# Forming mean, epsilon and scale of the norms on ScalarE instead of GpSimd, in a one-core hybrid conformer and attention block

## The chip, the cores and the metric

The kernel runs on one core of one Trainium2 chip. A core has a matrix engine (TensorE; PE in the profile, with its weight loads as PEld), VectorE (DVE), ScalarE (ACT), GpSimd (POOL) and a queue that issues DMAs (SyncE, SP). Each engine works through its own instructions in order; semaphores make one wait for another. The metric is the device time of one execution in microseconds, as the median of several.

## The reference, cut to what matters

One layer over 512 tokens of width 1024, everything in float32:

```python
h = rms_norm(x, g_pre_mix) * (1 + scale1) + shift1
z = h @ w_in                      # GLU | q latent | kv latent | rotary key | two gates
u = causal_depthwise_conv(glu)    # 31 taps
u = silu(layer_norm(u))           # over the 1024 channels
y_a = u @ w_conv_out
q = rms_norm(q_lat) @ w_uq ; kv = rms_norm(kv_lat) @ w_ukv
y_b = attention(q, kv) @ w_attn_out
y = (g_a * y_a + g_b * y_b) @ w_out
x = x + gate1 * rms_norm(y, g_post_mix)
h = rms_norm(x, g_pre_mlp) * (1 + scale2) + shift2
x = x + gate2 * rms_norm(relu(h @ w_mlp_in)**2 @ w_mlp_out, g_post_mlp)
# rms_norm: y * rsqrt(mean(y*y) + 1e-6) * g ;  layer_norm: (u - mean) * rsqrt(var + 1e-6) * g + b
```

So there are four kinds of RMS norm (of x, of the two latents, of the mixer's output and of the new x, of the MLP's output) and one layer norm.

## The kernel before, in words

Tokens are worked on in NT = 4 tiles of 128. Every large product is done as three float32r matmuls (high by high, high by low, low by high), for which ACT rounds each operand to its high part (a CAST) and DVE subtracts to get the low part. The work runs: norm of x; its transposes; first products with w_in; the latents and the rest of the GLU; attention over 8 heads; w_attn_out; the two gate products (GB, then GA); the layer norm of the convolution; w_conv_out; w_out; the post-mixer norm and the pre-MLP norm; the MLP in four chunks; the last norm and the output.

The 31-tap convolution runs on DVE as 248 multiply-adds of 128x512, each reading two operands from SBUF, spread through everything from the latents to the layer norm.

The order of instructions is not written by hand. `emit` records every operation with its regions read and written; `Planner.plan` simulates the five engines with the costs of `Planner.cost` and picks, for each engine, the ready operation with the earliest due time (for PE, the lowest rank; `plan.boost` moves operations ahead). It repeats this up to nine times with the buffer lifetimes of the pass before, keeps the shortest plan, and `issue` writes the instructions in that order. All of them come from line 388, so the profile tells them apart by tile and shape alone. In the planner's costs a small GpSimd operation is 160 ns (460 ns for a power), a small ACT operation 93 ns, and 150 ns pass until another engine may go on.

What the change touches:

- `rstd` (line 507): turns a sum of squares into 1/sqrt(sum*scale + base). GpSimd does a `tensor_scalar` (multiply, add) and then a `tensor_tensor` with the power -0.5. The sums come from ACT (`Square` with `accum_out`; in the trace an ACTIVATE followed by an ACTIVATION_READ_ACCUMULATOR). The consumers are DVE, except for the latents, where ACT multiplies.
- The two-part norms at lines 1381 and 1576: one GpSimd `tensor_scalar` forms the first half's sum times the scale plus epsilon (`s[:, 2:3]`), and `rstd` takes that as its base.
- `ln_stats` (line 1214): the statistics of the layer norm's first six channel blocks. For the first four, ACT copies the transposed block with `accum_out=sA`; GpSimd multiplies the sum by -1/512 into `ns`; ACT then squares with `ns` as its bias. PE's transposes for it are boosted (line 1270), so that they stand early in PE's order, between the matmuls of the gate products.
- `layer_norm` (line 1228) closes the statistics on DVE, takes one power of 128x4 on GpSimd, and forms the scale and shift that DVE and ACT apply.

Tiles by name: `stats` holds the sums of the RMS norms, `lns` those of the layer norm, `nhalf` the constant -0.5, `f_arena` and `r_arena` the float32 and float32r buffers.

Of the kernel before, what the change touches and what calls it, by code (L numbers as in the profile page):

```python
# [11 lines left out]
F32 = mybir.dt.float32  # L12
R32 = mybir.dt.float32r
I32 = mybir.dt.int32
AF = mybir.ActivationFunctionType
ALU = mybir.AluOpType

P = 128
T = 512
NT = T // P  # L20
D = 1024
# [371 lines left out]
def tile_hybrid_block(  # L393
# [35 lines left out]
    nc.gpsimd.memset(ones, 1.0)  # L429
    nhalf = const.tile([P, 8], F32, name="nhalf")  # L430
    nc.gpsimd.memset(nhalf, -0.5)
    mask = const.tile([P, T], F32, name="mask")
    nc.gpsimd.memset(mask, 0.0)
    nc.gpsimd.affine_select(out=mask[:, T - P:], in_=mask[:, T - P:], compare_op=ALU.is_ge, fill=1e30,
# [5 lines left out]
    def emit(past, replay):  # L440
# [63 lines left out]
            assert st_n[0] <= 96  # L504
            return st[:, a:a + n]

        def rstd(o, ssq, scale, base=EPS):

            n = o.shape[1]
            pool.tensor_scalar(o, ssq, scale, base, ALU.mult, ALU.add)  # L510
            pool.tensor_tensor(o, o, nhalf[:, :n], ALU.pow)


# [688 lines left out]
        pump(KD * TAPS)  # L1202
        vT = []

        lns = tile_of([P, 12, NT], F32, "lns")
        sA, ns, qA, dB, qB, dC, qC, dm, va, rs, nb, tq = (lns[:, i] for i in range(12))

        def ln_in(t, c0, n):
            b = pb.alloc()
# [4 lines left out]
        def ln_stats(c0, n, d, q):  # L1214

            for t in range(NT):
                b = ln_in(t, c0, n)
                j = ra.alloc(n * P)
                if d is None:
                    act.activation(ra.v(j), pb.v(b, n * P), AF.Copy, accum_out=sA[:, t:t + 1])  # L1220
                    pool.tensor_scalar(ns[:, t:t + 1], sA[:, t:t + 1], -1.0 / (n * P), None, ALU.mult)
                else:
                    act.activation(ra.v(j), pb.v(b, n * P), AF.Identity, bias=ns[:, t:t + 1], accum_out=d[:, t:t + 1])
                act.activation(ra.v(j), pb.v(b, n * P), AF.Square, bias=ns[:, t:t + 1], accum_out=q[:, t:t + 1])
                ra.free(j)
                pb.free(b)
# [142 lines left out]
        for tp in range(2):  # L1369
            xn = []  # L1370
            for t in (2 * tp, 2 * tp + 1):
                for k in range(KD):
                    mm3(pb.v(ys[t, 1]), yl(t, k), wo[k // 2](k % 2, 0, 512), k == 0, k == KD - 1)
                    if t == NT - 1 and k % 2 == 1:
                        wo[k // 2].free()
                s = stat(6)
                j = fa.alloc(512)
                for nh in range(2):
                    act.activation(fa.v(j), pb.v(ys[t, nh]), AF.Square, accum_out=s[:, nh:nh + 1])
                fa.free(j)  # L1380
                pool.tensor_scalar(s[:, 2:3], s[:, 0:1], 0.25 / D, EPS, ALU.mult, ALU.add)
                rstd(s[:, 3:4], s[:, 1:2], 0.25 / D, s[:, 2:3])
                y = fa.alloc(D)
                for nh in range(2):
                    sl = slice(nh * 512, (nh + 1) * 512)
                    dve.scalar_tensor_tensor(fa.v(y)[:, sl], pb.v(ys[t, nh]), s[:, 3:4], fa.v(G1)[:, sl], op0=ALU.mult, op1=ALU.mult)
                    pb.free(ys[t, nh])
                dve.tensor_tensor(fa.v(xr[t]), fa.v(xr[t]), fa.v(y), ALU.add)
                act.activation(fa.v(y), fa.v(xr[t]), AF.Square, accum_out=s[:, 4:5])
                rstd(s[:, 5:6], s[:, 4:5], 1.0 / D)  # L1390
                dve.tensor_scalar(fa.v(y), fa.v(xr[t]), s[:, 5:6], None, ALU.mult)
                sp.dma_start(out=xD[t], in_=fa.v(xr[t]))
                fa.free(xr[t])
                xn.append(y)
            if tp == 1:
                for m in mT:
                    ra.free(*m)
                ws0[0, 1] = wunit(w_mlp_in, 4, 0, 4, 256)
                ws0.update(hid_weights(0, 4, 2))
            if tp == 0:  # L1400
                h2[:] = [pair(T) for _ in range(KD)]
            hsl = slice(tp * 256, (tp + 1) * 256)
            for k2 in range(KD // 2):
                b = pb.alloc()
                for q in range(2):
                    for t in range(2):
                        k = 2 * k2 + q
                        pe.transpose(pb.v(b)[:, (2 * q + t) * P:(2 * q + t + 1) * P], fa.v(xn[t])[:, k * P:(k + 1) * P], ident)
                for q in range(2):
                    k = 2 * k2 + q  # L1410
                    ps, v = pb.v(b)[:, q * 256:(q + 1) * 256], fa.alloc(256)
                    hb, lb = h2[k]
                    if k == 0:
                        act.activation(ra.v(hb)[:, hsl], ps, AF.Identity, scale=mod[:, 3, k:k + 1], bias=mod[:, 2, k:k + 1])
                        dve.tensor_scalar(fa.v(v), ps, mod[:, 3, k:k + 1], mod[:, 2, k:k + 1], ALU.mult, ALU.add)
                    else:
                        act.activation(fa.v(v), ps, AF.Identity, scale=mod[:, 3, k:k + 1], bias=mod[:, 2, k:k + 1])
                        act.copy(ra.v(hb)[:, hsl], fa.v(v))
                    dve.tensor_tensor(ra.v(lb)[:, hsl], fa.v(v), rf(hb)[:, hsl], ALU.subtract)
                    fa.free(v)  # L1420
                pb.free(b)
            fa.free(*xn)
# [99 lines left out]
        for ch in range(NCH):  # L1522
# [32 lines left out]
            def banked(mi, nh, bs):  # L1555
# [3 lines left out]
                for tt in range(2):  # L1559
                    t = 2 * mi + tt  # L1560
                    y = fa.v(ysb[t])[:, sl]
                    if ch == 0 and n == 1:
                        act.copy(y, pb.v(bs[tt]))
                    else:
                        dve.tensor_tensor(y, pb.v(bs[tt]), y, ALU.add)
                    if ch < NCH - 1 or not done:
                        continue
                    s = fin[t]
                    i = seen[t] = seen.get(t, -1) + 1
                    j = ra.alloc(512)  # L1570
                    act.activation(ra.v(j), y, AF.Square, accum_out=s[:, i:i + 1])
                    ra.free(j)
                    dve.tensor_tensor(y, y, fa.v(G2)[:, sl], ALU.mult)
                    if i == 0:
                        continue
                    pool.tensor_scalar(s[:, 2:3], s[:, 0:1], 1.0 / D, EPS, ALU.mult, ALU.add)
                    rstd(s[:, 3:4], s[:, 1:2], 1.0 / D, s[:, 2:3])
                    xb = load(D, xD[t])
                    for hf in range(2):
                        sh = slice(hf * 512, (hf + 1) * 512)  # L1580
                        dve.scalar_tensor_tensor(fa.v(ysb[t])[:, sh], fa.v(ysb[t])[:, sh], s[:, 3:4], fa.v(xb)[:, sh],
                                                 op0=ALU.mult, op1=ALU.add)
                        sp.dma_start(out=out[t * P:(t + 1) * P, sh], in_=fa.v(ysb[t])[:, sh])
# [50 lines left out]
```

## Time and profile before

| | |
|---|---|
| median of 3 runs | 838.59 us (838.47 to 839.24) |
| the profiled execution | 836.4 us, its span 834.6 us |
| busy in the span | PE 808.1 us (97%), DVE 685.2 (82%), ACT 415.5 (50%), POOL 45.4 (5%) |
| DMA | 117.28 MB, mean 141 GB/s |
| chain that ended last | PE 85%, DMA 4%, DVE 3%, POOL 2%, ACT 2% |

The span is the time from the first to the last instruction on the core. Busy time is read by stage, because the share over the span averages stages with different limits; what counts for an edit is which engine PE was waiting for in the stage where the edit lies.

### The profile page before, as it was taken

The page shows a single profiled execution, that of the slowest core. Times are in us where ns is not written, and L with a number is a line of the kernel's source. Part 1 is how long each engine was busy: PE and PEld are TensorE (multiplying, and loading weights), DVE is VectorE, ACT ScalarE, POOL GpSimd, SP SyncE. Part 2 cuts the span into 40 slices and gives each one's busy share as a digit, 9 for nine tenths or more (in the row PEclk, how much of TensorE's full clock was granted, in tenths as well). Part 3 has the DMA queues.
Part 4 walks back from the last instruction along what each step waited for, and adds up shares of the span by engine and source line. Part 5 has one row for each costly group of instructions (what it writes and reads, how often), then busy time and mean ns, then how long its engine had stood idle before and what let it go on. Part 6 is the DMA issues. An engine that isn't in the chain of part 4 may idle for free.

```text
span 834.6 us, 10659 instructions
## 1 busy us (share of the span) xinstructions
PE 808.1 (97%) x3940; PEld 675.7 (81%) x3940; DVE 685.2 (82%) x1012; ACT 415.5 (50%) x680; POOL 45.4 (5%) x119
## 2 busy tenths in 40 slices
PE   6999999999999989999999989999999999999995
PEld 3777888899988868888888779888888888888884
DVE  4979979999999997999999779298529993975696
ACT  5463363375893346227434287375346544553641
POOL 3001040000000020000000230000000000000002
PEclk9999999999999999999999989999999999999998
DMA  9997423202353141332799650064014831660302
GB/s 310 336 311 234 148 69 98 67 27 77 101 177 102 51 128 49 101 111 91 233 353 363 210 201 27 26 202 152 0 51 132 290 132 51 197 206 1 101 1 101
DMA packets 86823, 117.28 MB, mean 141 GB/s; under 512 B 7274, under 2 KB 60627, under 8 KB 86770
## 3 DMA queue, kind: packets, MB, share of 16 engines
q1 hardware_dynamic: 86770, 116.59, 43.5%
q8 instruction: 31, 0.51, 0.2%
q14 instruction: 22, 0.18, 0.1%
HBM read 108.18 MB, written 8.39 MB: 140 GB/s over the span
## 4 chain that ended last, share of the span: by engine, by line
PE 85%; DMA 4%; DVE 3%; POOL 2%; issue 2%; ACT 2%; SPq 1%; DVEq 0%; POOLq 0%; ACTq 0%
PE psum L388 85%; DMA f_arena<-in_w_in_dram 4%; DVE f_arena L388 3%; SPq L388 1%; POOL stats L388 1%; ACT f_arena L388 1%; DMA f_arena<-in_x_dram 1%; ACT r_arena L388 1%; POOL lns L388 1%; DVE r_arena L388 0%; DVEq L1629 0%; POOLq L1629 0%; DMA rows<-in_kv_norm_g_dram 0%; DVE mod L388 0%; DVE cols L388 0%
## 5 line engine op out<-in xcount | busy, mean ns | idle before, releaser
L388 PE MATMUL psum<-r_arena 128*128 128x512 f32 (+2 forms) x3592 | 766.5, 374 | 4.0 <-ACT r_arena L388 2.5
L388 PEld LDWEIGHTS psum<-r_arena 128*128 128x128 f32 x3592 | 634.4, 190 | 121.0 <-ACT r_arena L388 3.6
L388 DVE TENSOR_TENSOR r_arena<-f_arena,r_arena 128x1024 fp32r<-128x1024 f32 (+4 forms) x232 | 247.9, 1090 | 97.1 <-PE psum L388 48.5
L388 ACT CAST r_arena<-f_arena 128x1024 fp32r<-128x1024 f32 (+4 forms) x222 | 209.7, 966 | 183.3 <-PE psum L388 111.5
L388 DVE SCALAR_TENSOR_TENSOR f_arena<-f_arena,cw 128x512 f32<-128x512 f32 x240 | 164.8, 743 | 0.0
L388 ACT ACTIVATE f_arena<-psum 128x512 f32<-128x512 f32 x64 | 38.0, 597 | 119.6 <-PE psum L388 111.3
L388 DVE TENSOR_TENSOR f_arena<-f_arena 128x1024 f32<-128x1024 f32 (+3 forms) x78 | 77.0, 1003 | 8.3 <-ACT f_arena L388 6.3
L388 ACT ACTIVATE f_arena<-f_arena 128x512 f32<-128x512 f32 (+3 forms) x100 | 58.5, 604 | 20.2 <-DVE f_arena L388 19.4
L388 DVE SCALAR_TENSOR_TENSOR f_arena<-f_arena,cT 128x256 f32<-128x256 f32 (+2 forms) x84 | 55.2, 699 | 0.1
L388 PE MATMUL psum<-ident,f_arena 128*128 128x128 f32 (+1 forms) x240 | 35.3, 288 | 11.7 <-DVE f_arena L388 7.7
L388 PEld LDWEIGHTS psum<-ident,f_arena 128*128 128x128 f32 (+1 forms) x240 | 29.2, 148 | 17.2 <-DVE f_arena L388 8.7
L388 POOL TENSOR_SCALAR stats<-stats 128x1 f32<-128x1 f32 x32 | 14.8, 463 | 467.0 <-ACT r_arena L388 361.6
L388 DVE TENSOR_TENSOR f_arena<-psum,f_arena 128x512 f32<-128x512 f32 x52 | 35.2, 684 | 4.2 <-PE psum L388 3.9
L388 ACT CAST r_arena<-psum 128x512 fp32r<-128x512 f32 (+2 forms) x57 | 30.2, 566 | 15.8 <-PE psum L388 15.4
L388 DVE TENSOR_TENSOR r_arena<-psum,r_arena 128x512 fp32r<-128x512 f32 (+2 forms) x57 | 35.7, 656 | 2.2 <-ACT r_arena L388 1.9
L388 ACT COPY f_arena<-psum 128x512 f32<-128x512 f32 (+4 forms) x42 | 19.9, 500 | 23.0 <-PE psum L388 22.7
L388 ACT ACTIVATE r_arena<-f_arena 128x512 fp32r<-128x512 f32 (+3 forms) x20 | 13.0, 648 | 21.9 <-DVE f_arena L388 18.8
L388 DVE CUSTOM_DVE_ANT_0 f_arena<-psum,mask 128x128 f32<-128x128 f32 (+3 forms) x32 | 15.0, 484 | 2.5 <-PE psum L388 2.5
L388 POOL TENSOR_SCALAR lns<-lns 128x1 f32<-128x1 f32 x4 | 5.3, 1326 | 198.5 <-ACT r_arena L388 198.5
L388 POOL TENSOR_TENSOR stats<-stats,nhalf 128x1 f32<-128x1 f32 x24 | 15.2, 633 | 1.9
L388 DVE TENSOR_SCALAR f_arena<-f_arena,stats 128x1024 f32<-128x1024 f32 x8 | 6.0, 754 | 9.9 <-POOL stats L388 9.7
L388 DVE SCALAR_TENSOR_TENSOR f_arena<-f_arena 128x512 f32<-128x512 f32 (+1 forms) x18 | 13.1, 742 | 0.0
(93 smaller groups left out, 195.4 us busy)
## 6 DMA issues: line engine op xcount, KB each, us to landing
f_arena<-in_w_ada_dram SPq DMA_DIRECT2D x16, 1024.0 KB, 5.6
f_arena<-in_w_mlp_in_dram SPq DMA_DIRECT2D x32, 512.0 KB, 5.1
f_arena<-in_w_mlp_out_dram SPq DMA_DIRECT2D x32, 512.0 KB, 5.2
f_arena<-in_w_in_dram SPq DMA_DIRECT2D x28, 512.0 KB, 4.9
f_arena<-in_x_dram SPq DMA_DIRECT2D x8, 512.0 KB, 5.3
f_arena<-in_w_ada_dram SPq DMA_DIRECT2D x16, 256.0 KB, 5.7
f_arena<-in_w_ada_dram SPq DMA_DIRECT2D x8, 512.0 KB, 6.7
h_spill<-r_arena SPq DMA_DIRECT2D x16, 256.0 KB, 5.4
```

Source lines behind the costliest of these rows:

```text
L388: getattr(self.real[o.eng], o.fn)(*o.a, **o.k)
```

## The change

GpSimd keeps the power alone; scaling and adding epsilon go to ACT as an `Identity` activation with a scale and a bias read from SBUF, directly behind the accumulation that made the sum. A constant tile `epsc` holds epsilon. In the layer norm's statistics the factor -1/512 goes into the copy itself, so that its accumulated sum is the negative mean and no operation follows.

```diff
+    epsc = const.tile([P, 1], F32, name="epsc")
+    nc.gpsimd.memset(epsc, EPS)
...
-        def rstd(o, ssq, scale, base=EPS):
+        def rstd(o, ssq, scale, base=None):
             n = o.shape[1]
-            pool.tensor_scalar(o, ssq, scale, base, ALU.mult, ALU.add)
+            act.activation(o, ssq, AF.Identity, scale=scale, bias=epsc[:, 0:1] if base is None else base)
             pool.tensor_tensor(o, o, nhalf[:, :n], ALU.pow)
...
                 if d is None:
-                    act.activation(ra.v(j), pb.v(b, n * P), AF.Copy, accum_out=sA[:, t:t + 1])
-                    pool.tensor_scalar(ns[:, t:t + 1], sA[:, t:t + 1], -1.0 / (n * P), None, ALU.mult)
+                    act.activation(ra.v(j), pb.v(b, n * P), AF.Copy, scale=-1.0 / (n * P), accum_out=ns[:, t:t + 1])
...
-                pool.tensor_scalar(s[:, 2:3], s[:, 0:1], 0.25 / D, EPS, ALU.mult, ALU.add)
+                act.activation(s[:, 2:3], s[:, 0:1], AF.Identity, scale=0.25 / D, bias=epsc[:, 0:1])
                 rstd(s[:, 3:4], s[:, 1:2], 0.25 / D, s[:, 2:3])
...
-                    pool.tensor_scalar(s[:, 2:3], s[:, 0:1], 1.0 / D, EPS, ALU.mult, ALU.add)
+                    act.activation(s[:, 2:3], s[:, 0:1], AF.Identity, scale=1.0 / D, bias=epsc[:, 0:1])
                     rstd(s[:, 3:4], s[:, 1:2], 1.0 / D, s[:, 2:3])
```

The tile `lns` loses its row `sA`. Nothing else in the source is changed, but the planner lays out every engine's order anew.

## Rows read from the trace of the kernel before

**Rows 1.** Busy time by stage: stretch, length, engines (instructions), PE clock, DMA share, GB/s.

```profile
0.00:68.00 68.00, 59.17 (x270) 43.61 (x270) 50.02 (x119) 36.81 (x52) 7.75 (x58) 1.00 1.00 313
68.00:247.00 179.00, 178.72 (x1044) 157.94 (x1044) 166.54 (x329) 99.03 (x217) 12.46 (x24) 1.00 0.35 107
306.00:313.00 7.00, 3.00 (x16) 2.17 (x16) 5.42 (x8) 2.13 (x6) 4.62 (x1) 1.00 0.06 7
463.00:493.00 30.00, 27.18 (x128) 21.68 (x128) 21.74 (x30) 14.61 (x34) 8.27 (x15) 0.97 0.56 187
493.00:816.00 323.00, 323.00 (x1509) 271.88 (x1509) 235.25 (x238) 166.40 (x211) 3.27 (x6) 0.99 0.34 107
```

**Rows 2.** Timeline at the first layer-norm statistics: start, length, instructions [idle before, releaser].

```profile
302.26 8.03 DVE L388 SCALAR_TENSOR_TENSOR f_arena<-f_arena,cw 128x512 f32<-128x512 f32 x12
306.62 0.20 ACT L388 ACTIVATION_READ_ACCUMULATOR r_arena<-psum 128x1 f32 x1
306.90 4.62 POOL L388 TENSOR_SCALAR lns<-lns 128x1 f32<-128x1 f32 x1 [191.51 <-ACT r_arena L388]
310.21 1.22 DVE L388 TENSOR_TENSOR r_arena<-f_arena,r_arena 128x1024 fp32r<-128x1024 f32 x1
311.56 0.69 ACT L388 ACTIVATE r_arena<-psum,lns 128x512 fp32r<-128x512 f32 x1 [4.74 <-POOL lns L388]
312.39 1.14 PE L388 MATMUL psum<-ident,f_arena 128*128 128x128 f32 x8 [4.00 <-ACT r_arena L388]
316.29 1.23 DVE L388 TENSOR_TENSOR r_arena<-f_arena,r_arena 128x1024 fp32r<-128x1024 f32 x1 [4.87 <-ACT r_arena L388]
```

**Rows 3.** The stretch right behind that wait, columns as in rows 1.

```profile
312.39:318.00 5.61, 5.61 (x24) 4.58 (x25) 1.71 (x3) 3.87 (x10) 0.41 (x2) 0.70 0.34 93
```

**Rows 4.** Timeline of GpSimd alone, later in the span.

```profile
379.40 2.03 POOL L388 TENSOR_TENSOR lns<-lns,nhalf 128x4 f32<-128x4 f32 x1 [60.24 <-DVE lns L388]
...
807.84 0.19 POOL L388 TENSOR_SCALAR stats<-stats 128x1 f32<-128x1 f32 x1 [309.61 <-ACT r_arena L388]
```

**Rows 5.** Groups of instructions by form, of GpSimd and of ACT: busy, mean ns.

```profile
L388 POOL TENSOR_SCALAR stats<-stats 128x1 f32<-128x1 f32 x32 | 14.8, 463 | 467.0 <-ACT r_arena L388 361.6 <-ACT f_arena L388 103.7 <-ACT tmp L388 0.6
...
L388 ACT ACTIVATE f_arena<-ident,lns 128x128 f32<-128x128 f32 x4 | 1.3, 390 | 0.6 <-DVE lns L388 0.6
...
L388 ACT ACTIVATE tmp<-cT 128x8 f32<-128x8 f32 x1 | 0.2, 193 | 0.0
```

**Rows 6.** Timeline at the end of the layer norm.

```profile
366.26 4.71 DVE L388 SCALAR_TENSOR_TENSOR f_arena<-f_arena,cw 128x512 f32<-128x512 f32 x7
...
372.17 0.60 PE L388 MATMUL psum<-ident,f_arena 128*128 128x128 f32 x4
...
379.23 1.29 DVE L388 SCALAR_TENSOR_TENSOR f_arena<-f_arena 128x512 f32<-128x512 f32 x2
...
381.46 0.28 DVE L388 TENSOR_SCALAR f_arena<-ident,lns 128x128 f32<-128x128 f32 x1 [0.94 <-POOL lns L388]
...
381.89 2.02 PE L388 MATMUL psum<-f_arena,ones 128*128 128x128 f32 x16
```

**Rows 7.** Two stretches around the pre-MLP norm, columns as in rows 1.

```profile
488.00:493.00 5.00, 2.58 (x11) 1.65 (x10) 3.93 (x6) 5.00 (x15) 2.59 (x4) 0.82 0.79 260
491.00:498.20 7.20, 6.65 (x30) 6.25 (x31) 5.76 (x11) 6.77 (x13) 2.85 (x4) 0.53 0.73 254
```

**Rows 8.** Timeline of the last norm, up to the last DVE work.

```profile
828.00 0.19 ACT L388 ACTIVATION_READ_ACCUMULATOR r_arena<-f_arena 128x1 f32 x1
828.22 0.69 DVE L388 TENSOR_TENSOR f_arena<-f_arena 128x512 f32<-128x512 f32 x1 [0.79 <-ACT r_arena L388]
828.29 0.76 POOL L388 TENSOR_SCALAR stats<-stats 128x1 f32<-128x1 f32 x1 [3.65 <-ACT r_arena L388]
829.13 0.54 POOL L388 TENSOR_TENSOR stats<-stats,nhalf 128x1 f32<-128x1 f32 x1
829.71 1.42 DVE L388 SCALAR_TENSOR_TENSOR f_arena<-f_arena,stats 128x512 f32<-128x512 f32 x2 [0.79 <-POOL stats L388]
```

More of the change, by code (lines that the diff above doesn't have):

```diff
@@ L1203, in emit @@
         vT = []
-        lns = tile_of([P, 12, NT], F32, "lns")
-        sA, ns, qA, dB, qB, dC, qC, dm, va, rs, nb, tq = (lns[:, i] for i in range(12))
+        lns = tile_of([P, 11, NT], F32, "lns")
+        ns, qA, dB, qB, dC, qC, dm, va, rs, nb, tq = (lns[:, i] for i in range(11))
         def ln_in(t, c0, n):
```

## Prediction, made before the result was known

> **What bounds the kernel.** I first read busy time stage by stage [rows 1]. From 68 us on, PE is the kernel: it works 178.72 of 179.00 us through the latents and attention, and all 323.00 us of the MLP. Nothing done for ACT or GpSimd in such a stage can move the end. Four places are left: the first 68 us, where the DMA share is 1.00 and PE works 59.17 us; the seven microseconds from 306 to 313, where PE works only 3.00; the post-mixer and pre-MLP norms from 463 to 493, where it works 27.18 of 30.00; and the tail after the last matmul.
>
> Next I read the timeline of the odd seven microseconds [rows 2]. ACT finishes the sum of the first 128x512 block at 306.82. GpSimd takes it at 306.90 and needs 4.62 us for one multiplication of 128x1. ACT waits 4.74 us for that, PE 4.00 us for ACT (its transposes need what ACT holds), and DVE afterwards 4.87 us for ACT. Why 4.62? The 32 operations of the same form on `stats` take 0.46 us in the mean [rows 5], and one takes 0.19. What runs beside it is DVE: twelve multiply-adds with two operands in SBUF without a gap from 302.26 to 310.29, then a subtraction with two such operands to 311.43. GpSimd ends at 311.52, 0.09 us behind the last of them. So I read the 4.62 us as GpSimd kept out while DVE runs two-operand instructions back to back.
>
> What marks this place is the consumer. `ns` is consumed by ACT, so DVE has no reason to stop. Almost all the powers are consumed by DVE, which reaches the consumer in its own order, stops, and lets GpSimd in: the power at 379.40 took 2.03 us [rows 4], with DVE's filler (1.29 us from 379.23) in front and DVE idle 0.94 us behind it [rows 6].
>
> **The change part by part.** Thirty-six GpSimd multiplications go: 32 on `stats`, 4 on `lns`. Thirty-two become ACT activations of 128x1; the 4 become a scale inside a copy that ACT makes anyway, at nothing.
>
> *The mean of the layer norm.* ACT goes from sum to square without leaving its queue: start at about 306.85 instead of 311.56, 4.71 us earlier. PE's transposes, at 312.39 minus 4.71 = 307.68, would then be ready before PE is through with its earlier matmuls (312.39 - 4.00 = 308.39), with 0.71 us to spare. PE's whole wait goes: **4.00 us**. A lower end is the same wait cut to nothing by something else that is late next (rival C).
>
> Behind the wait PE pays again: from 312.39 to 318.00 its granted clock is 0.70 on average [rows 3], between its levels of 2.4 and 1.2 GHz, after 4.00 us in which it did nothing. It loses 0.30 x 5.61 = **1.68 us** of full-speed work, which I take back as well.
>
> Does it last? PE comes to the end of the layer norm 5.7 us earlier, 372.17 to 366.5 [rows 6]. DVE must have finished the convolution by then; it does so at 370.97 now, and moves by its lost 4.87 us (less about 0.1, since its subtraction before ends at 311.43 in any case): 366.2. That just holds. What comes behind is set by PE and by buffers that DVE or PE free, not by a fixed time, so I let it move along whole.
>
> *The chains of `rstd`.* From row to row this is a trade. Taken away: a GpSimd operation of 0.19 us (unhindered) plus about 0.09 until the next. Added: an ACT activation of 128x1 with a bias from SBUF, which no row shows. From below, 128x8 without such an operand takes 0.193 us [rows 5]; from above, 128x128 with one takes 0.390, of which a part is the 128 elements. I take 0.28, nearer the middle, since one element a lane and one such operand lie between. The trade is 0.28 against 0.28: nothing. Where GpSimd was kept out by DVE, the power now meets the same DVE instruction, and only what ran behind it is gained.
>
> The Trainium skill (ScalarE: Activation LUTs, section What ACT_TABLE_LOAD costs) gives 186 ns plus 0.833 ns an element for an ACTIVATE and about 93 ns more for each [128,1] operand. By it the new activation would be an estimated 0.28 us, and by its section Rules for kernel authors, such adds and multiplies would go to VectorE, not ScalarE. By those figures the trade is also about zero on the path; it is ACT's queue that pays.
>
> *ACT's queue.* The new activations wait only for ACT's own sums, so no other engine's lateness gets in front of what is queued behind them (CASTs and evacuations). They cost room: 32 x 0.19 to 0.28 = 6 to 9 us on an engine busy half of the span. In the first stage (four) DMA covers them; uncovered they would cost 1.1 us. For the latents (eight) PE's 178.72 of 179.00 us does; uncovered 2.2 us.
>
> *From 463 to 493* the cover is thin. PE loses 2.82 us there [rows 1], and from 491.0 to 498.2 its granted clock is 0.53, a loss of 0.47 x 7.20 = 3.4 us [rows 7]. Twelve activations are added. ACT works all 5.00 us from 488 to 493, when PE waits for its CASTs; the six activations of the last two tiles could hold PE up by 6 x 0.28 = 1.7 us if all stand in front. In the other direction, GpSimd's two back-to-back chains lose an operation each. I take zero, with +1.7 and, if every wait and the slow clock went, -6.2 as ends.
>
> *The tail.* In the last chain [rows 8] ACT's sum is ready at 828.19, GpSimd multiplies until 829.05 (held up by DVE's two-operand multiply, 828.22 to 828.91), the power runs to 829.67 and DVE resumes at 829.71. With the factor on ACT (828.2 to 828.5), the power meets that DVE multiply and can have its 0.54 us from 828.91: 829.45. Gain **0.22 us**; from below 0 (an activation that takes 0.390 and a power that waits longer), from above 0.6.
>
> *The tile `epsc`* is one more GpSimd memset among those of the first 3 us, under the load of x: nothing.
>
> **Sum.** 4.00 + 1.68 + 0.22 = 5.9 us. The profiled execution, 836.4 us (span 834.6 and 1.8 around it), becomes 830.5; the median of the runs, 838.59, lies 2.2 above that execution and becomes **832.7 us**.
>
> **The rivals.**
>
> A. *The slow clock of 491 to 498 goes as well.* PE's pauses there add up to 2.4 us from 488 to 493 [rows 7]; a little less waiting could leave the clock up. For it: GpSimd's chains are shorter where they queue. Against it: ACT is full there and gets more work. Up to 6.2 us more: 826.5 to 831.
>
> B. *The 4.62 us is a cold start and is only moved.* GpSimd had been idle 191.51 us. Then the power of 128x4 at 379.40 becomes its first work and takes 4.62 us instead of 2.03. PE's matmuls that follow (381.89) show no wait before them now, so PE pays 2.6 us, perhaps with 1.7 of slow clock: 832.7 + 2.6 to 4.3 = 835.3 to 837.0. Against it: after 309.61 us of idleness GpSimd needs 0.19 us [rows 4], and at 306.90 it ended with DVE. The rule nearest to my reading is that of the Trainium skill (SBUF — State Buffer, section Who interferes with whom): a DVE instruction with two SBUF inputs and a GpSimd instruction that reads SBUF exclude each other, and the second to issue blocks until the first finishes. The trace agrees in kind, but by the letter one multiply-add of 0.7 us would be the whole block, and the other 3.7 us would be something else, such as B. The row shows a block through the entire run of them, which decides for me.
>
> C. *DVE becomes the bound.* If DVE's 4.87 us is not recovered, or the new order spends it on other work, PE meets the convolution's end at 370.97 instead of 372.17 and gains 1.2 us, with the tail 1.4: 837.2 (the clock may still fall). For it: DVE runs without a gap from 302.26 to 311.43 [rows 2] and for 4.71 us up to that end [rows 6]. A reshuffled order that makes PE wait once elsewhere ends here too: 836.9 to 840.3.
>
> D. *Slower: the power at the layer norm's end is shut out.* It is the one GpSimd operation left on PE's path there, with no slack before 381.89. If the planner, which charges it 0.46 us, queues more DVE work before the consumer, PE waits for each piece. The two short multiply-adds of 1.29 us there now cost nothing; five of the modulation's multiply-adds of about 1.28 us would cost 6.4 us of waiting and 1.7 of slow clock, 8.1 in all, against 5.9 gained: 840.8 and more. It decides from the fifth on. Against it: an order with the same costs but for a few small ones has no reason to put five there.
>
> **How the numbers follow.** Forecast 0.58, A 0.10, B 0.07, C 0.14, D 0.11. The likeliest is 832.7, alone from 831.0 to 834.6 (the tail's and the norms' bounds). The range leaves out the far half of A and most of D, and takes in C: 828.5 to 839.0. About 0.2% (1.7 us) is what a measurement of this kernel can tell from no change: 836.9 to 840.3 counts as the same. Forecast, A and B are faster, 0.75; C is the same, 0.14; D slower, 0.11.
>
> **What would show it.** Right: ACT's square starts within 0.1 us of its sum at the first layer-norm block; PE has no wait of more than 1 us between 300 and 380 and its clock stays at 1.00 there; no `tensor_scalar` on `lns` or `stats`; ACT activations of 128x1, 0.19 to 0.39 us each; the power of 128x4 at about 2 us, ending with a DVE run. Wrong: a wait of PE of 2 us or more before the layer norm's final matmuls (B, D) or before the last transposes of the convolution (C); new waits of PE in the MLP, where it has none; or more idle time from 463 to 500.

## The result, and the profile after

The changed kernel takes 832.51 us (median of 4, 830.56 to 833.03) against 838.80 us for the kernel before in the same series (4 runs, 838.47 to 839.24): a ratio of 0.992, 95% interval 0.9903 to 0.9938. Its profiled execution took 832.68 us with a span of 830.9. The chain that ended last is PE for 87% (85% before), and GpSimd's share of 2% rounds to 0%.

First the windows by stage of the changed kernel (stretch, length, busy time of PE, PEld, DVE, ACT and POOL, PE clock, DMA share, GB/s), the same stretches as [rows 1, 3, 7] with one more, 380 to 460:

```profile
0.00:68.00 68.00, 57.44 (x265) 42.55 (x266) 48.55 (x116) 37.13 (x56) 6.68 (x55) 1.00 0.98 308
306.00:313.00 7.00, 7.00 (x40) 5.63 (x40) 7.00 (x12) 5.58 (x14) 0.00 (x0) 1.00 0.00 0
312.39:318.00 5.61, 5.61 (x32) 4.58 (x31) 5.61 (x9) 5.54 (x18) 0.00 (x0) 1.00 0.09 9
380.00:460.00 80.00, 77.22 (x335) 62.85 (x335) 75.24 (x95) 38.76 (x51) 0.00 (x0) 0.98 0.79 281
463.00:493.00 30.00, 27.32 (x139) 22.36 (x138) 18.84 (x26) 17.63 (x47) 5.39 (x7) 1.00 0.37 126
491.00:498.20 7.20, 7.20 (x60) 6.99 (x59) 7.13 (x12) 7.20 (x16) 1.39 (x2) 1.00 0.73 257
```

The odd seven microseconds are full (PE 7.00, was 3.00) and the clock behind them is 1.00 (was 0.70). The slow clock from 491 to 498 is gone as well (1.00, was 0.53), which was rival A. But PE works 1.73 us less in the first 68 us, and a stage that had no loss before has one now. This is the window 380 to 460 of the kernel before:

```profile
380.00:460.00 80.00, 79.96 (x363) 66.15 (x362) 75.46 (x100) 41.67 (x58) 1.43 (x1) 1.00 0.75 265
```

PE loses 2.74 us there. The timeline of the changed kernel at the first layer-norm statistics and at the layer norm's end (start, length, instructions, idle before and its releaser), against [rows 2, 4]:

```profile
302.36 9.36 DVE L388 SCALAR_TENSOR_TENSOR f_arena<-f_arena,cw 128x512 f32<-128x512 f32 x14
...
308.11 0.20 ACT L388 ACTIVATION_READ_ACCUMULATOR r_arena<-psum 128x1 f32 x1
308.33 0.69 ACT L388 ACTIVATE r_arena<-psum,lns 128x512 fp32r<-128x512 f32 x1
...
309.26 0.60 PE L388 MATMUL psum<-ident,f_arena 128*128 128x128 f32 x4
...
371.13 1.40 POOL L388 TENSOR_TENSOR lns<-lns,nhalf 128x4 f32<-128x4 f32 x1 [256.18 <-DVE lns L388]
```

ACT's square follows 0.02 us behind the end of its sum (4.74 us before). PE's transposes have no wait. DVE still runs its multiply-adds from 302 to 312, and no engine waits for GpSimd meanwhile. The power, now GpSimd's first work after 256.18 us of idleness, takes 1.40 us, so a cold start of some 4 us did not move there.

Where PE now waits, from the timelines of PE and ACT of the changed kernel:

```profile
436.19 1.57 ACT L388 CAST r_arena<-f_arena 128x1024 fp32r<-128x1024 f32 x2 [1.89 <-DMA f_arena<-in_w_out_dram]
...
437.29 1.20 PE L388 MATMUL psum<-r_arena 128*128 128x512 f32 x4 [2.44 <-ACT r_arena L388]
...
487.79 1.07 ACT L388 ACTIVATE f_arena<-f_arena 128x1024 f32<-128x1024 f32 x1
488.75 0.20 ACT L388 ACTIVATION_READ_ACCUMULATOR f_arena<-f_arena 128x1 f32 x1
488.84 0.59 ACT L388 ACTIVATE f_arena<-psum 128x512 f32<-128x512 f32 x1
...
490.09 1.02 ACT L388 ACTIVATE f_arena<-psum,mod 128x256 f32<-128x256 f32 x2
...
490.70 1.10 PE L388 MATMUL psum<-r_arena 128*128 128x256 f32 x7 [2.43 <-ACT f_arena L388]
```

At 437 PE waits 2.44 us for a CAST that waits for a weight of w_out. At 490 it waits 2.43 us: in ACT's order the evacuations at 490.09 stand behind two squares with their sums and two of the new activations. The tail, from the timeline, against [rows 8]:

```profile
824.62 0.19 ACT L388 ACTIVATION_READ_ACCUMULATOR r_arena<-f_arena 128x1 f32 x1
824.84 0.29 ACT L388 ACTIVATE stats<-stats 128x1 f32<-128x1 f32 x1
824.84 0.69 DVE L388 TENSOR_TENSOR f_arena<-f_arena 128x512 f32<-128x512 f32 x1 [0.79 <-ACT r_arena L388]
825.22 0.73 POOL L388 TENSOR_TENSOR stats<-stats,nhalf 128x1 f32<-128x1 f32 x1 [3.90 <-ACT stats L388]
825.98 1.41 DVE L388 SCALAR_TENSOR_TENSOR f_arena<-f_arena,stats 128x512 f32<-128x512 f32 x2 [0.44 <-POOL stats L388]
```

From the end of the last sum to DVE's next work it is 1.17 us (825.98 - 824.81), before 1.52 (829.71 - 828.19). At last the groups of the new activations, by form (busy, mean ns, idle before):

```profile
L388 ACT ACTIVATE stats<-stats,epsc 128x1 f32<-128x1 f32 x24 | 6.5, 291 | 0.3
...
L388 ACT ACTIVATE stats<-stats 128x1 f32<-128x1 f32 x8 | 2.4, 296 | 0.2
```

So the number is right, but two gains that I had not counted (the clock at 491, part of the tail) and two losses that I had not counted (at 437, and the first stage) lie in it. Is that one change, or two that cancel? The change edits operations, and it also makes the planner lay the order anew. The experiments take these apart.

### The profile page after: what moved, and what is told of

Its sections match the earlier page's. It is cut to its first block, busy times and chain, and to the rows that moved or that the text cites. A ratio compares the mean times of both kernels' runs of the same rounds, so it can differ in the third digit from the quotient of the medians.

```text
span 830.9 us, 10647 instructions
## 1 busy us (share of the span) xinstructions
PE 805.1 (97%) x3940; PEld 672.5 (81%) x3940; DVE 686.6 (83%) x1012; ACT 422.4 (51%) x712; POOL 26.4 (3%) x84
## 4 chain that ended last, share of the span: by engine, by line
PE 87%; DVE 6%; DMA 4%; ACT 2%; issue 1%; POOL 0%; POOLq 0%; DVEq 0%; ACTq 0%; SPq 0%
PE psum L388 87%; DVE f_arena L388 4%; DMA f_arena<-in_w_in_dram 2%; DVE r_arena L388 1%; ACT f_arena L388 1%; DMA f_arena<-in_w_out_dram 1%; ACT r_arena L388 1%; POOL stats L388 0%; DMA f_arena<-in_x_dram 0%; DMA f_arena<-in_w_ada_dram 0%; ACT stats L388 0%; POOLq L1630 0%; DVE mod L388 0%; DVEq L1630 0%; DVE cols L388 0%
## 5 line engine op out<-in xcount | busy, mean ns | idle before, releaser
L388 PE MATMUL psum<-r_arena 128*128 128x512 f32 (+3 forms) x3592 | 765.7, 373 | 8.5 <-ACT r_arena L388 3.6
L388 DVE SCALAR_TENSOR_TENSOR f_arena<-f_arena,psum 128x512 f32<-128x512 f32 x16 | 11.0, 685 | 3.1 <-PE psum L388 2.6
L388 DVE SCALAR_TENSOR_TENSOR f_arena<-psum,stats,f_arena 128x512 f32<-128x512 f32 x8 | 5.6, 748 | 8.5 <-POOL stats L388 8.3
```

Source lines behind the costliest of these rows:

```text
L388: getattr(self.real[o.eng], o.fn)(*o.a, **o.k)
```

## The experiments

Twelve runs were made in three series: ten other kernels, and two of the kernels a second time. Each series ran on one chip with its own runs of the kernel before (medians 837.82 us of 23 runs, 837.06 of 11, 837.17 of 11). The ratios below are to these runs, with a 95% interval.

### Half of the change at a time, with the planner free

The fold of the mean alone:

```diff
-  act.activation(ra.v(j), pb.v(b, n * P), AF.Copy, accum_out=sA[:, t:t + 1])
-  pool.tensor_scalar(ns[:, t:t + 1], sA[:, t:t + 1], -1.0 / (n * P), None, ALU.mult)
+  act.activation(ra.v(j), pb.v(b, n * P), AF.Copy, scale=-1.0 / (n * P), accum_out=ns[:, t:t + 1])
```

> Only the mean's factor goes into the copy; rstd and the bases stay on GpSimd; the planner lays out a new order. Theory 1 (the gain is the wait for the mean, 4.0 us of PE, and the slow clock behind it, 1.7): 838.8 - 5.7 = 833.1 us, with up to 3 us either way from the new order, and no wait of PE over 1 us from 300 to 380. Theory 2 (the gain is the shorter chains of rstd or the new order as such): within 1.7 us of 838.8.

And the rest of it alone (`rstd` and the two bases on ACT, the mean as before):

```diff
-            pool.tensor_scalar(o, ssq, scale, base, ALU.mult, ALU.add)
+            act.activation(o, ssq, AF.Identity, scale=scale, bias=epsc[:, 0:1] if base is None else base)
...
-                pool.tensor_scalar(s[:, 2:3], s[:, 0:1], 0.25 / D, EPS, ALU.mult, ALU.add)
+                act.activation(s[:, 2:3], s[:, 0:1], AF.Identity, scale=0.25 / D, bias=epsc[:, 0:1])
...
-                    pool.tensor_scalar(s[:, 2:3], s[:, 0:1], 1.0 / D, EPS, ALU.mult, ALU.add)
+                    act.activation(s[:, 2:3], s[:, 0:1], AF.Identity, scale=1.0 / D, bias=epsc[:, 0:1])
```

> Only rstd and the bases go to ACT; the mean's multiplication stays on GpSimd; new order. Theory 1: PE still waits some 4 us for the mean behind a run of DVE multiply-adds and the clock falls behind it, so 838.6 us, up to 3 either way from the new order. Theory 2: most of the change's 6.3 us is here, 832 to 834 us.

The fold alone took 837.96 us (12 runs): 1.0001, interval 0.9989 to 1.0013. Nothing of the 5.7 us came out, so by its time alone theory 2 holds. The other half took 836.71 us (12 runs): 0.9991, interval 0.9977 to 1.0005. There theory 1 holds: PE still waits for the mean, whose multiplication takes 4.57 us:

```profile
312.50 1.81 PE L388 MATMUL psum<-ident,f_arena 128*128 128x128 f32 x8 [3.94 <-ACT r_arena L388]
```

And the fold did its work all the same: from 300 to 380 PE is busy 79.84 of 80.00 us at a clock of 1.00. The loss stands elsewhere. PE's waits with the fold alone, from its timeline:

```profile
418.38 1.20 PE L388 MATMUL psum<-r_arena 128*128 128x512 f32 x4 [0.95 <-ACT r_arena L388]
...
422.70 13.32 PE L388 MATMUL psum<-r_arena 128*128 128x512 f32 x48 [3.12 <-DVE r_arena L388]
...
492.74 1.08 PE L388 MATMUL psum<-r_arena 128*128 128x256 f32 x4 [1.68 <-ACT r_arena L388]
```

Before, nothing of that kind stood between 380 and 460 (79.96 of 80.00). An edit that removes a wait whole and leaves the time where it was points to the order.

### The same edits in the order of before

The planner plans the old operations, and the new ones are issued in their places; where a GpSimd operation has been folded away its place stays empty. No other instruction moves.

```diff
-        for o in order:
-            getattr(self.real[o.eng], o.fn)(*o.a, **o.k)
+        for eng, fn, a, k in [o.swap or (o.eng, o.fn, o.a, o.k) for o in order if o.swap != ()]:
+            getattr(self.real[eng], fn)(*a, **k)
```

The fold of the mean alone in this way:

```diff
+                    plan.ops[-1].swap = ("act", "activation", (ra.v(j), pb.v(b, n * P), AF.Copy),
+                                         dict(scale=-1.0 / (n * P), accum_out=ns[:, t:t + 1]))
                     pool.tensor_scalar(ns[:, t:t + 1], sA[:, t:t + 1], -1.0 / (n * P), None, ALU.mult)
+                    plan.ops[-1].swap = ()
```

> The mean's factor in the copy, but every engine's instructions in exactly the order (and the buffers in the places) of the kernel before; the four GpSimd multiplications are left out and nothing else differs. Theory 1: 838.8 - 5.7 = 833.1 us (832.3 to 834.1), the wait of 4.00 us before PE's transposes gone, the granted clock 1.00 from 300 to 380. Theory 2: within 1.7 us of 838.8. Theory 3 (cold start of GpSimd, moved): the power of 128x4 takes 4 to 5 us and PE waits 2 to 3 us before the layer norm's last matmuls, 835 to 837 us.

All edits in this way, with the old call planned and the new one issued:

```diff
             pool.tensor_scalar(o, ssq, scale, base, ALU.mult, ALU.add)
+            plan.ops[-1].swap = ("act", "activation", (o, ssq, AF.Identity),
+                                 dict(scale=scale, bias=epsc[:, 0:1] if base is EPS else base))
```

> All edits of the change with the order of the kernel before: the ACT activations stand where the GpSimd multiplications were planned. Theory 1: as with the mean alone, less 0.2 us for the tail: 832.9 us; from 463 to 498 between 1.7 us more (ACT's queue) and 6.2 less (PE's waits and the slow clock). Theory 2: at least 1.5 us below the run with the mean alone.

The fold took 831.35 us (6 runs, 830.55 to 832.72): 0.9925, interval 0.9909 to 0.9941, so 6.5 us off its 837.82. All edits took 828.34 us (5 runs, 827.19 to 829.92): 0.9889, interval 0.9871 to 0.9907, another 3.0 us. The two kernels' runs don't overlap. The first part is my mean (5.68 predicted). The second part I had put at 0.22; here theory 2 held. Where it comes from is seen in PE's waits from 460 to 500, first with the fold alone, then with all edits:

```profile
473.69 0.33 PE L388 MATMUL psum<-ident,f_arena 128*128 128x128 f32 x1 [0.43 <-DVE f_arena L388]
...
485.50 1.08 PE L388 MATMUL psum<-r_arena 128*128 128x256 f32 x4 [1.69 <-ACT r_arena L388]
486.84 0.66 PE L388 MATMUL psum<-ident,f_arena 128*128 128x128 f32 x4 [0.26 <-DVE f_arena L388]
...
488.39 8.00 PE L388 MATMUL psum<-r_arena 128*128 128x256 f32 x52 [0.90 <-DVE f_arena L388]
```

```profile
478.41 1.53 PE L388 MATMUL psum<-ident,f_arena 128*128 128x128 f32 x12 [0.25 <-DVE f_arena L388]
...
484.40 1.08 PE L388 MATMUL psum<-r_arena 128*128 128x256 f32 x4 [1.58 <-ACT r_arena L388]
...
486.12 0.69 PE L388 MATMUL psum<-ident,f_arena 128*128 128x128 f32 x2 [0.16 <-ACT f_arena L388]
```

That is 3.28 against 1.99 us. The tail gives more: from PE's last matmul to DVE's last string it is 5.56 us with the fold alone (819.29 to 824.85) and 4.39 with all edits (817.22 to 821.61). 1.3 and 1.2 make 2.5 of the 3.0 us. The two profiled executions differ by 3.2 us (831.52 and 828.34); in the first, PE is already 0.91 us behind at 248 us (248.71 against 247.80), where, as shown below, two executions of one kernel differ by as much and more. So of the 3.0 us some 2.5 are seen to come of the edits, and the rest can't be told from such scatter.

### Is it DVE's run that keeps GpSimd out?

The sum rests on one reading: GpSimd's 4.62 us were DVE's run. Rival B said a cold start. The run is longer than the twelve multiply-adds that [rows 2] show, because that timeline begins inside it: DVE's own timeline has sixteen without a gap, from 299.61 to 310.29. Two kernels change nothing but the length of that run. In the first, six multiply-adds with a factor of zero are appended to it:

```diff
+        run = self.conv_run(order); more = {run[-1].i: [run[-2], run[-1]] * 3}
...
+        a = o.a if o.i not in self.seen else o.a[:2] + (self.zero,) + o.a[3:]
```

> The kernel before, but six more multiply-adds (repeats with a factor of zero, so the output stays) stand at the end of VectorE's run of convolution multiply-adds at 302 to 310 us, about 0.67 us each, so the run ends some 4.0 us later. Shut out by the run (my reading): GpSimd's one multiplication for the layer norm's mean takes about 8.6 us instead of 4.62, it still ends within 0.1 us of the end of the run, PE waits about 8 us instead of 4.00, and the kernel is about 4 us slower, perhaps 5 with the clock. Cold start (the rival): the multiplication takes 4.6 us as before and ends in the middle of the run; PE's wait there stays at 4.0; the kernel is slower by at most what VectorE's added 4 us cost later, 0 to 4 us.

In the second, its last twelve multiply-adds are left out, which leaves four:

```diff
+        skip = {o.i for o in self.conv_run(order)[-12:]}
+        for o in [p for p in order if p.i not in skip]: getattr(self.real[o.eng], o.fn)(*o.a, **o.k)
```

> The kernel before, with the last twelve convolution multiply-adds of VectorE's run at 302 to 310 us left out (the output changes by these twelve of 248 multiply-adds). Shut out by the run (my reading): VectorE has nothing but its subtraction of 1.2 us there, the multiplication for the mean takes 0.2 to 1.4 us instead of 4.62, PE's wait of 4.00 us is gone, its clock stays at 1.00, and the kernel is about 5.7 us faster (4.00 and 1.68 of clock), 832. Cold start (the rival): the multiplication still takes 4.6 us, PE's wait stays at about 4 us and the time at 837 to 838.

The longer run took 841.24 us (8 runs, against 837.06): 1.0045, interval 1.0033 to 1.0058. Its timeline of DVE, GpSimd and PE:

```profile
300.51 10.68 DVE L404 SCALAR_TENSOR_TENSOR f_arena<-f_arena,cw 128x512 f32<-128x512 f32 x16
...
307.81 8.59 POOL L404 TENSOR_SCALAR lns<-lns 128x1 f32<-128x1 f32 x1 [191.49 <-ACT r_arena L404]
...
311.12 4.05 DVE L404 SCALAR_TENSOR_TENSOR f_arena<-f_arena,mask 128x512 f32<-128x512 f32 x6
315.09 1.22 DVE L404 TENSOR_TENSOR r_arena<-f_arena,r_arena 128x1024 fp32r<-128x1024 f32 x1
...
317.27 1.97 PE L404 MATMUL psum<-ident,f_arena 128*128 128x128 f32 x8 [7.97 <-ACT r_arena L404]
```

DVE's run is 4.0 us longer, GpSimd's one multiplication takes 8.59 us instead of 4.62 and ends at 316.40, 0.09 us behind DVE's subtraction, as before. PE waits 7.97 instead of 4.00, and the kernel pays it (4.2 us by the medians). The shorter run took 831.19 us (4 runs): 0.9921, interval 0.9904 to 0.9939. Its timeline:

```profile
300.56 2.73 DVE L388 SCALAR_TENSOR_TENSOR f_arena<-f_arena,cw 128x512 f32<-128x512 f32 x4
...
307.86 0.24 POOL L388 TENSOR_SCALAR lns<-lns 128x1 f32<-128x1 f32 x1 [191.48 <-ACT r_arena L388]
308.13 0.69 ACT L388 ACTIVATE r_arena<-psum,lns 128x512 fp32r<-128x512 f32 x1 [0.36 <-POOL lns L388]
```

The same instruction, after the same 191.48 us of idleness, takes 0.24 us when DVE stands still (idle from 303.29 to 308.76). That settles B. The Trainium skill (SBUF — State Buffer, section Who interferes with whom) has the lock between GpSimd and a DVE instruction with two SBUF inputs. The traces agree that there is one, but here the block did not last for one such instruction: it lasted through all the 0.67 us instructions that followed without a gap. (It does not always; the last section has the cases.)

The gain of the shorter run, 0.9921, is that of the fold in the old order, 0.9925, within the intervals (5.9 and 6.5 us by the medians): two ways to be rid of the wait give the same, though the shorter run also takes 8 us of work from DVE. So the 5.7 us of the forecast were the right term, and about the right size.

### What an order is worth

If the order matters that much, a new order of the old operations must move the time too. Here only a price of the planner differs:

```diff
-        return (460.0 if ALU.pow in self.args else 160.0) + 1.0 * n, 150.0
+        return (460.0 if ALU.pow in self.args else 400.0) + 1.0 * n, 150.0
```

> The kernel before, with the same operations; only the planner's price of a small GpSimd operation other than the power is 400 ns instead of 160, so it lays out the order anew. If the order that the planner happens to lay is worth some 4 us either way (my reading of the change and of the fold of the mean alone): the time moves by 2 us or more in either direction, 830 to 836 or 840 to 845, and PE shows waits of over 1 us at other places than before. If a new order is worth little (the rival: the loss against the old order comes from the added ScalarE work in the queue): 836.5 to 839.2, and PE's waits stay where they are.

And here the order of the changed kernel is kept and the old operations are put back into it:

```diff
+            plan.ops[-1].swap = [("pool", "tensor_scalar", (o, ssq, scale, EPS if base is None else base, ALU.mult, ALU.add), {})]
...
+                    plan.ops[-1].swap = [
+                        ("act", "activation", (ra.v(j), pb.v(b, n * P), AF.Copy), dict(accum_out=sA[:, t:t + 1])),
+                        ("pool", "tensor_scalar", (ns[:, t:t + 1], sA[:, t:t + 1], -1.0 / (n * P), None, ALU.mult), {})]
```

> The order of the changed kernel, instruction by instruction, but with the old operations: at each place of a new ScalarE activation of 128x1 stands the GpSimd multiplication, and the sum of the layer norm is again multiplied by GpSimd behind its copy. If the order costs about 4 us by itself whatever the operations (my reading): the old operations in it give 841 to 843, with PE's wait of about 4 us for the mean back at 308 to 312 and the waits for weights of over 1 us at about 437 and 490 us still there. If the added work on ScalarE is what brings those waits (the rival): they are gone, and the time is that of the kernel before, 837 to 839.

The first took 846.28 us (4 runs): 1.0104, interval 1.0089 to 1.0119, slower by more than I gave it. PE's long waits are not at other places, as I had expected, but at the old one: the new order puts a longer run of DVE beside the mean.

```profile
307.15 12.11 POOL L388 TENSOR_SCALAR lns<-lns 128x1 f32<-128x1 f32 x1 [191.44 <-ACT r_arena L388]
...
307.34 10.68 DVE L388 SCALAR_TENSOR_TENSOR f_arena<-f_arena,cw 128x512 f32<-128x512 f32 x16
317.94 1.22 DVE L388 TENSOR_TENSOR r_arena<-f_arena,r_arena 128x1024 fp32r<-128x1024 f32 x1
...
320.12 1.97 PE L388 MATMUL psum<-ident,f_arena 128*128 128x128 f32 x8 [11.26 <-ACT r_arena L388]
```

A second wait for the mean, 3.31 us, follows at 329; from 380 to 460 PE is busy 79.81 of 80.00 us. So this order costs time through the same shut-out, made longer.

The second took 849.08 us (4 runs): 1.0134, interval 1.0117 to 1.0151. I had expected 841 to 843, with one mean shut out. Three were:

```profile
307.79 3.83 POOL L388 TENSOR_SCALAR lns<-sA 128x1 f32<-128x1 f32 x1 [191.10 <-ACT r_arena L388]
313.95 1.95 POOL L388 TENSOR_SCALAR lns<-sA 128x1 f32<-128x1 f32 x1 [2.33 <-ACT r_arena L388]
317.37 6.48 POOL L388 TENSOR_SCALAR lns<-sA 128x1 f32<-128x1 f32 x1 [1.47 <-ACT r_arena L388]
```

PE waits for them twice, 3.65 and 5.62 us. The later waits of the changed kernel are there too, some 12 us later in the span. This is the window 380 to 460, and PE's wait behind it:

```profile
380.00:460.00 80.00, 77.21 (x350) 63.30 (x349) 74.72 (x108) 38.79 (x55) 1.43 (x1) 1.00 0.66 236
...
502.42 1.09 PE L388 MATMUL psum<-r_arena 128*128 128x256 f32 x7 [2.09 <-ACT f_arena L388]
```

PE is busy 77.21 of 80.00 us, as in the changed kernel (77.22), with the waits for w_out at 449 and 452. The wait in front of the seven matmuls at 490.70 (2.43 us there) is 2.09 us here, behind the same evacuations, which again stand behind two squares and their sums in ACT's order; only the two new activations are not in it. So both losses belong to the order: they are there with the old operations as well, and ACT's added work accounts for some 0.3 us of the second. That half of the expectation held. In all, PE's waits of the norms are 3.83 us here (496 to 505).

Last, new orders for the new operations, with the changed kernel and the old order again beside them. First, a ScalarE operation on one element priced 93 ns higher:

```diff
-            t = 0.833 * n + (51 if psum else 93) + 93 * scalars
+            t = 0.833 * n + (51 if psum else 93) + 93 * scalars + (93 if n == 1 else 0)
```

> The changed kernel, with the planner's price of a ScalarE operation on one element a lane raised by 93 ns, so it lays out the order anew; the operations are the same. If a new order of the new operations scatters as one of the old operations did (846 and 849 where the old order gave 837): 828 to 845, and PE has waits of over 1 us at other places than 437 and 490 us. If the new operations make the order less dear, because no GpSimd multiplication stands between two ScalarE operations any more (my reading): PE has no wait in the layer norm from 300 to 330, what is left is one to three waits of 1 to 3 us elsewhere, and the time is 828 to 836.

Then the power priced at 900 ns instead of 460:

```diff
-        return (460.0 if ALU.pow in self.args else 160.0) + 1.0 * n, 150.0
+        return (900.0 if ALU.pow in self.args else 160.0) + 1.0 * n, 150.0
```

> The changed kernel, with the planner's price of a GpSimd power raised from 460 to 900 ns, so it lays out the order anew; the operations are the same. By my reading (the new operations bound what an order can cost): no wait of PE from 300 to 330, one to three waits of 1 to 3 us elsewhere, 828 to 836. By the rival (orders scatter the same whatever the operations): any time from 828 to 849, with a wait of over 3 us at one place.

And the two again, unchanged:

> The changed kernel as it is, beside the two orders above and the next on one chip: 831 to 834; its waits at about 437 and 490 us are there again if they belong to the order, and not to this one execution.

> All the changed operations at the old order's places, beside the changed kernel on one chip: 827 to 830, so 3 to 5 us faster than the changed kernel, if the order is what costs it that. If the difference came of two chips or of a lucky profile: within 1.7 us of the changed kernel.

| kernel, all new operations (before: 837.17) | median us | runs | ratio to before, interval |
|---|---|---|---|
| the changed kernel | 831.58 | 6 | 0.9937, 0.9916 to 0.9959 |
| one-element ScalarE price up | 830.87 | 5 | 0.9923, 0.9904 to 0.9941 |
| power price up | 829.41 | 4 | 0.9905, 0.9880 to 0.9929 |
| order of before | 828.42 | 6 | 0.9899, 0.9878 to 0.9920 |

All four are faster than before, within 3.2 us of one another; three orders of the old operations lie at 837, 846 and 849, the last one laid out for other operations than it carries. None of the four has a wait of PE from 300 to 330. With the one-element price PE has two waits of over 1 us, 1.39 at 484 and 1.57 at 487, as I expected. With the price of the power it has one, and that is over the 3 us that I allowed:

```profile
486.07 0.94 PE L388 MATMUL psum<-r_arena 128*128 128x256 f32 x2 [3.34 <-DVE f_arena L388]
```

DVE's work in front of it waits for a power that took 1.59 us (482.89 to 484.48), so the powers left on GpSimd can still be held up. My bound on a single wait did not hold; the bound on the time did (829.41). The difference of 3.2 us between the first row and the last came out as expected, though their runs overlap by a microsecond (830.12 to 834.70, and 827.25 to 831.20). The waits at 437 and 490 are there again, so they don't belong to one execution; this is the timeline of PE of the changed kernel's second profile:

```profile
438.04 4.83 PE L388 MATMUL psum<-r_arena 128*128 128x512 f32 x20 [2.21 <-DVE r_arena L388]
...
488.41 1.86 PE L388 MATMUL psum<-r_arena 128*128 128x256 f32 x7 [2.43 <-ACT f_arena L388]
```

The four together are not proof that every order of the new operations is good: the fold alone, with the planner free, came to 837.96. The best kernel of the study is the new operations in the order of before: 828.34 and 828.42 in its two series.

## Why the prediction was right, and where it was not

The time of 832.7 us was met (832.51), and the faster side with it. That it was met so closely is luck: the largest term is right, but two terms that I had put at about nothing are 3 us each, with opposite signs.

| term | predicted gain, us | measured gain, us | from |
|---|---|---|---|
| PE's wait for the mean, with its clock | 5.68 | 6.5 | fold in the old order, 837.82 to 831.35 |
| the chains of `rstd`, tail included | 0.22 | 3.0 | all edits in the old order, 831.35 to 828.34 |
| the order laid anew | 0 | -3.2 | old order to changed kernel, 828.42 to 831.58 |
| sum | 5.9 | 6.3 | the change as a whole: 6.3 (838.80 to 832.51) and 5.6 (837.17 to 831.58) |

The measured terms come from two series on two chips, so their sum is good to about a microsecond.

*The mean of the layer norm.* Right in place, cause and nearly in size. The wait of 4.00 us is gone in every kernel with the fold. In those without it, except the one with the shorter run, it is there, and its length goes with what DVE runs (3.94, 7.97 and 11.26 us, or 3.65 and 5.62). The clock behind it stays at 1.00 in the changed kernel and with the fold in the old order; in the latter the excess of 0.8 us over the sum is within the interval (gain of 4.9 to 7.6). DVE's lost time came back as I worked it out: PE has no wait from 300 to 380. That DVE would have stopped for GpSimd if the consumer had been its own is a reading that no run tested.

*The chains of `rstd`.* The price of the new activation was right: 0.28 us taken, 0.291 and 0.296 measured. (The estimate from the Trainium skill, ScalarE: Activation LUTs, section What ACT_TABLE_LOAD costs, was 0.28 us too; the trace agrees.) The step that failed is "the trade is 0.28 against 0.28: nothing". I traded a GpSimd multiplication at its free price of 0.19 us, while [rows 5] give a mean of 0.463, so many of them are held up as well: in the kernel before, three from 488 to 498 took 0.70, 0.82 and 1.59 us, and that of the last chain 0.76. In the tail that counted for 0.36 us in the last chain (0.22 predicted) and 0.8 more in the chains ahead of it, which I had not looked at. From 463 to 493, "I take zero" was wrong by 1.3 us of waiting (460 to 500), well inside the bounds that I kept (+1.7 and -6.2).

*The new order.* "What comes behind ... I let it move along whole" is the other step that failed. The planner laid every queue anew, and the order that it found costs 3.2 us against the old one: PE runs out of weights at 437 (2.7 us lost from 380 to 460, none in the old order), and at 490 ACT has the statistics in front of an evacuation (PE's waits of the norms are 2.68 us, 1.99 in the old order). That is rival C's "reshuffled order that makes PE wait once elsewhere", with two waits. It did not take the gain because the 3.0 us of `rstd` stood beside it. The fold alone, replanned, shows what C looks like when they don't: 837.96, inside C's 836.9 to 840.3.

*The rivals.* A happened in the profiled execution (the clock of 1.00 from 491 to 498) but not for the reason given: PE's waits of 463 to 493 are hardly shorter (2.68 us, 2.82 before), and in the second profile the clock from 490 to 500 was 0.92. B fell by the two kernels with another run. D did not come: the power took 1.40 us (I had expected about 2) and PE did not wait for it.

*The first stage.* PE's 1.73 us less up to 68 us need not be the change's. One kernel in two executions (the order of before with all edits) started the same matmuls behind the latents at 247.80 and at 250.22; before and after differ less, 247.31 and 248.81.

What stays open is why the planner's new order brings w_out's weights too late at 437: that the order does it is shown, by which move was not tried.

## What to carry to other kernels

A small GpSimd operation can cost what DVE happens to run beside it, not its own length: look for the one that another engine than DVE waits for while DVE has a long run of work, and fold its work into an instruction of the engine that made its input. Where a planner or a scheduler lays out the order, time an edit also in the old order with only its own instructions exchanged; without that, here, a gain of 6.5 us reads as nothing (837.96) and one of 8.7 as 5.6 (837.17 to 828.42 and 831.58). A forecast for such a change needs a term for the order, with both signs.

## What the runs showed of the hardware

*How long GpSimd is kept out.* Often for longer than one DVE instruction. Multiplications of 128x1 that take 0.19 to 0.28 us alone took 1.95, 3.83, 4.57, 4.62, 6.48, 8.59 and 12.11 us. Where DVE's subtraction followed the run without a gap (five of these seven), GpSimd was not done at the end of the last multiply-add either, but 0.07 to 0.10 us behind the end of the subtraction: in the order with the price of 400 ns at 319.26, with DVE's subtraction of 317.94 ending at 319.16, though the next multiply-adds began at 319.08.

But a run does not always keep it out. In the same kernel a multiplication came in behind the first of twelve multiply-adds without a gap:

```profile
331.17 8.04 DVE L388 SCALAR_TENSOR_TENSOR f_arena<-f_arena,cw 128x512 f32<-128x512 f32 x12
...
331.30 0.68 POOL L388 TENSOR_SCALAR lns<-lns 128x1 f32<-128x1 f32 x1 [2.62 <-ACT r_arena L388]
```

It ended at 331.98, seven microseconds before the run did. In the kernel before, the one at 318.89 ended at 319.16, between the two multiply-adds of 318.35 to 319.76. Both began while the first multiply-add of their run was at work, and in these traces that goes with it: what began beside the first multiply-add of a run of the convolution, or in one case the second, came in beside or behind that one; what began beside the third (317.37, 6.48 us), the fifth (322.17) or a later one (306.90, beside the twelfth of sixteen) stayed out to the end of the run. Nobody moved the start on purpose, so that this decides is not shown, nor what lets GpSimd in behind the subtraction.

*Where the clock falls.* One kernel can have its slow clock at different places in different executions. The changed kernel had 0.86 from 434 to 446 in the first profile and 1.00 in the second, with PE busy 9.29 and 9.22 of 12.00 us; and from 490 to 500 it had 1.00 and 0.92. So the gain of rival A, read from one profile, is partly luck, and a term for the clock behind a short wait (2.2 to 2.4 us here) needs more than one execution. Behind the long waits it fell each time: from 300 to 380 it was 0.98 with a wait of 4.00 us, 0.94 with one of 7.97, 0.87 with waits of 11.26 and 3.31, and 1.00 with none.
